# Silu of the values' compressor from Exp and VectorE operations, and one weight load queued behind the first copy of compressed keys, in a transformer block

## The chip, the cores and the metric

The kernel runs on one core of a Trainium2 chip. The core has TensorE (PE in the profile; its weight loads are listed apart as PEld), VectorE (DVE), ScalarE (ACT), GpSimd (POOL) and SyncE (SP), whose queue issues most DMAs. The metric is the device time of one execution in microseconds (us). Before the change the median of 3 runs is 960.73 us (960.63 to 961.4).

## The reference

One layer of a "macaron" transformer on 512 tokens of width 1024, all in float32:

- x = x + 0.5 * swiglu(rmsnorm(x)), a feed-forward part with hidden width 2816;
- x = x + mixer(rmsnorm(x)), the attention part;
- x = x + 0.5 * swiglu(rmsnorm(x)), and a last rmsnorm.

The mixer projects x to queries, keys and values of two families of eight heads. The first family (MoBA, heads 0 to 7 in the kernel) attends causally. The second (NSA, heads 8 to 15) adds three attentions under gates: over selected blocks, over a window, and over compressed keys and values. The compressor is what the change touches:

```
def compress(raw, pos, w1, w2):
    blocks = raw[:, :, idx] + pos
    return jax.nn.silu(blocks.reshape(B, G, n_cmp, NSA_CMP_LEN * dh) @ w1) @ w2

k_cmp = compress(kc_raw, pos_k, w1_k, w2_k)
v_cmp = compress(vc_raw, pos_v, w1_v, w2_v)
```

It is run once for the keys and once for the values: windows of 32 tokens, a hidden layer of 256, Silu, and a second matrix to 64 columns. Silu(h) is h / (1 + exp(-h)).

## The kernel before

Activations lie transposed, features on the partitions, in eight tiles of 128x512. Each float32 matrix product is made of three products of rounded halves: a value is split into a rounded copy (hi, by a Copy on ScalarE, line 95 for weights) and the rest (lo, by a subtraction on VectorE or GpSimd, lines 97 and 99), and `mm3` (lines 106 to 108) multiplies hi by hi, hi by lo and lo by hi.

The program has three phases: the first feed-forward part, the mixer and the second feed-forward part. The change is in the mixer. There two kinds of work are woven together by hand:

- Attention steps: logits of one head (line 1070), softmax (lines 1078 to 1087: sum with the bias and row minimum on VectorE, Exp on ScalarE, reciprocal of the sum on VectorE, scaling on GpSimd), transposes of the probabilities (line 1106) and the product with the values (lines 121 and 122).
- A stream of jobs that need a weight, such as the projections. The list `pre` is worked off before the attention begins, `fill` between its steps. `pre` ends with ... `ksec[1], nq[0], *vhid, nq[1]` and `fill` begins with `vsec[0], mq[0], vsec[1], nq[2]`. Here ksec and vsec are the second halves of the compressors of keys and values, vhid the values' hidden layer, nq and mq the projections of the queries of the NSA and MoBA heads. Within `stream`, `taken` loads up to three jobs ahead of the one that is worked on: `load` (line 75) fills one of four buffers `raw` by a DMA from SP, and `halves` splits it.

`need(("n", 1))` runs the stream until the query projection nq[1] is in; then the attention steps begin, and `run` advances the stream between them at a fixed rate.

What sets the order on each engine: the program is traced in the order of the Python code, and at the build a scheduler orders the instructions of each engine by a timeline of its own, the earlier in the program the sooner. `tc.issue_after(x)` adds an ordering edge: the instructions traced inside it, those on the same engine as x, come behind x on that engine. `held` uses it to keep the stream's matmuls behind the latest attention matmul. SP's queue, as each engine's, is worked off in order; an issue that waits holds what stands behind it.

In `compress`, `hidden` ends with lines 863 to 865: hid is the sum of two halves of the product in PSUM (a Copy on ScalarE, then the sum on VectorE), and Silu is applied on ScalarE, in place, on 64x256. ScalarE has tables for its functions, and the trace shows an ACT_TABLE_LOAD where a function needs another table. `turned` transposes hid on TensorE (line 874) and splits it (lines 880 and 881). `second` makes the second product; for the keys it writes the compressed keys of both groups into kst and copies them to the other 64 partitions by DMA, two copies for each group (lines 898 and 899, SP). kst[0] and kst[2], of the first group, are read by the logits of heads 8 to 11, kst[1] and kst[3] by those of heads 12 to 15. For the values it builds a tile vc and copies it by three DMAs (line 915).

The query of a head, aq, is made by lines 721 (ScalarE) and 722 (VectorE) from the scaled projection (line 715). Tiles with the tag "t" (scaled projections, hid, the lo half of the turned hid) share six buffers.

Of the kernel before, what the change touches and what calls it, by code (L numbers as in the profile page):

```python
# [9 lines left out]
F32 = mybir.dt.float32  # L10
F32R = mybir.dt.float32r
AF = mybir.ActivationFunctionType
ALU = mybir.AluOpType
# [16 lines left out]
def block_kernel(ctx: ExitStack, tc: tile.TileContext, A: dict, out: bass.AP):  # L30
# [7 lines left out]
    nc = tc.nc  # L38
# [16 lines left out]
    def f32(ap):  # L55
        return ap.bitcast(F32)
# [12 lines left out]
    def chunk(shape):  # L69
        raw = wp.tile([128, 1024], F32, name="raw", tag="raw", bufs=4)  # L70
        return raw[:, :shape[0] * shape[1]].rearrange("p (a b) -> p a b", a=shape[0])

    def load(src):
        v = chunk(src.shape[1:])
        nc.sync.dma_start(v, src)
        return halves(v, 48 if src.shape[-1] == HT else 0)
# [537 lines left out]
    with ExitStack() as ph:  # L614
        tmp = ph.enter_context(tc.tile_pool(name="tmp1", bufs=5))
# [64 lines left out]
    with ExitStack() as ph:  # L680
        tmp = ph.enter_context(tc.tile_pool(name="tmp2", bufs=2))
# [3 lines left out]
        def half(i):  # L685
            return slice(i * 64, i * 64 + 64)
# [23 lines left out]
        def scaled(p, by):  # L710
            t = tmp.tile([128, S], F32, name="t", tag="t", bufs=6)
            if by is None:
                nc.vector.tensor_tensor(t, p, R, ALU.mult)
            else:
                nc.vector.scalar_tensor_tensor(t, p, by, R, ALU.mult, ALU.mult)
            return t
# [94 lines left out]
                return src[:, k0:k1], body  # L811
            return [chunk_of(k0) for k0 in range(0, NK, per)]

        vm = []

        def vm_tiles():
            if not vm:
# [7 lines left out]
        def compress(which):  # L825

            xc, p = [], []
            tag = ("t", "mm")[which]

            def blocks(p):  # L830
                tv = scaled(p, None).rearrange("p (n s) -> p s n", s=16)
                xt = chunk((16, 64))
                xv = xt.rearrange("p l (g n) -> p l g n", g=2)
                nc.gpsimd.memset(xv[:, :, :, 31:32], 0.0)
                for g in range(2):
                    for l in range(2):
                        for e in range(2):
                            nc.vector.tensor_tensor(
                                xv[half(l), 8 * e:8 * e + 8, g, 0:31], tv[half(g), l:16:2, e:e + 31],
                                pos[half(g), which, 16 * e + l:16 * e + 16:2].unsqueeze(2).to_broadcast([64, 8, 31]),  # L840
                                ALU.add)
                for l0 in range(0, 16, 4):
                    t = akt().rearrange("p (l e n) -> p l e n", l=4, e=2)
                    nc.scalar.activation(t[:, :, 0], xt[:, l0:l0 + 4], AF.Copy)
                    nc.vector.tensor_tensor(t[:, :, 1], xt[:, l0:l0 + 4], f32(t[:, :, 0]), ALU.subtract)
                    xc.extend(t[:, l].rearrange("p e n -> p (e n)") for l in range(4))

            def hidden(c):
                def body(w):
                    if c == 0:  # L850
                        p.append(pt("mm", "pc"))
                    for l in range(4):
                        x, n = xc[c + l], c + l
                        with held():
                            if n:
                                nc.tensor.matmul(p[0][:64, :256], x[:, :64], w[l][1], start=False, stop=False)
                            newest[0] = nc.tensor.matmul(p[0][:, :256], x, w[l][0], start=n == 0, stop=n == 15)
                            if not n:
                                nc.tensor.matmul(p[0][:64, :256], x[:, :64], w[l][1], start=False, stop=False)
                        yield  # L860
                    if c == 12:
                        hid = tmp.tile([64, 256], F32, name="hid", tag="t", bufs=6)
                        nc.scalar.activation(hid, p[0][64:, :256], AF.Copy)
                        nc.vector.tensor_tensor(hid, p[0][:64, :256], hid, ALU.add)
                        nc.scalar.activation(hid, hid, AF.Silu)
                        p.append(hid)
                return A["w1"][which][:, c:c + 4], body

            def turned(w):
                hid = p[1]  # L870
                pp = pt(tag, "pct")
                for c in range(2):
                    with held():
                        nc.tensor.transpose(pp[:, c * 64:(c + 1) * 64], hid[:, c * 128:(c + 1) * 128],
                                            ident[:64, :64])
                yield
                hh = tmp.tile([128, 2, 64], F32R, name="hh", tag="hh", bufs=1)
                hl = tmp.tile([128, 2, 64], F32R, name="hl", tag="t", bufs=6)
                pv = pp[:, :128].rearrange("p (a b) -> p a b", a=2)
                nc.scalar.activation(hh, pv, AF.Copy)  # L880
                nc.vector.tensor_tensor(hl, pv, f32(hh), ALU.subtract)
                p.append((hh, hl))

            def second(w):
                hh, hl = p[2]
                pp = pt(tag, "pck")
                if which == 0:
                    for c in range(2):
                        with held():
                            mm3(pp[:64, :64], w[c], (hh[:, c], hl[:, c]), c == 0, c == 1)  # L890
                    yield
                    lo, hi = slice(0, CK), slice(CK, 2 * CK)
                    for g in range(2):
                        v, h, l = pp[:64, g * CK:(g + 1) * CK], kst[g], kst[2 + g]
                        nc.scalar.activation(h[0:64, hi], v, AF.Copy)
                        for to in (l[0:64, hi], h[0:64, lo]):
                            nc.vector.tensor_tensor(to, v, f32(h[0:64, hi]), ALU.subtract)
                        nc.sync.dma_start(f32(h[64:128, :2 * CK]), f32(h[0:64, :2 * CK]))
                        nc.sync.dma_start(f32(l[64:128, hi]), f32(l[0:64, hi]))
                    got["kc"] = True  # L900
                    return
                for g in range(2):
                    b = slice(g * 32, (g + 1) * 32)
                    for c in range(2):
                        with held():
                            mm3(pp[:32, g * 64:(g + 1) * 64], (hh[:, c, b], hl[:, c, b]), w[c], c == 0, c == 1)
                yield
                pv = pp[:32, :128].rearrange("p (a b) -> p a b", a=2)

                a = kv.tile([128, 2, 2, 2, 64], F32R, name="vc")  # L910
                nc.gpsimd.memset(f32(a), 0.0)
                nc.scalar.activation(a[:32, 0, :, 0], pv, AF.Copy)
                nc.vector.tensor_tensor(a[:32, 0, :, 1], pv, f32(a[:32, 0, :, 0]), ALU.subtract)
                for r, odd in ((2, 0), (1, 1), (3, 1)):
                    nc.sync.dma_start(f32(a[r * 32:(r + 1) * 32, odd]), f32(a[0:32, 0]))
                got["vc"] = a

            return (proj(8 + which, blocks), [hidden(c) for c in range(0, 16, 4)],
                    ((None, turned), (A["w2"][which], second)))
# [26 lines left out]
        def stream(jobs, ahead=3):  # L946

            jobs, loaded = list(jobs), []

            def taken():  # L950
                while jobs and len(loaded) <= ahead:
                    src, body = jobs.pop(0)
                    loaded.append((None if src is None else load(src), body))
                w, body = loaded.pop(0)
                return body(w), body

            while jobs or loaded:
                steps, body = taken()
                if body not in [job[1] for job in swapped]:
                    yield from steps  # L960
                    continue
                for _ in range(NK - 1):
                    next(steps)
                    yield
                more, _ = taken()
                for one in (more, steps):
                    next(one)
                    latest[0] = newest[0]
                    yield
                yield from steps  # L970
                yield from more
# [207 lines left out]
        mq, mk = [[proj(2 * i + j, moba_t(kind, i)) for i in range(4)] for j, kind in enumerate("qk")]  # L1179
# [71 lines left out]
    with ExitStack() as ph:  # L1251
        tmp = ph.enter_context(tc.tile_pool(name="tmp3", bufs=5))
# [201 lines left out]
```

## Time and profile before

| what | value |
| --- | --- |
| median of 3 runs | 960.73 us (960.63 to 961.4) |
| profiled execution, its own time | 960.46 us |
| its span, from the first to the last instruction | 958.7 us |
| PE, PEld, DVE, ACT, POOL busy | 949.7, 879.8, 764.6, 563.2, 163.2 us |
| mean granted TensorE clock | 0.998 |
| table loads on ScalarE, all and in the stretch from 383 to 425 us | 11 and 4, 1.28 us each |

All other times are those of the profiled execution, in us from the start of its span. "L865" is line 865 of the kernel before. In a timeline row stand the start, the duration, the engine, the line, the operation, the output and inputs by the program's names, the shape and the number of merged instructions (the duration is then that of all of them together, and the name that of the first); in brackets the idle time of the engine just before and what ended it. An engine with a q is its sequencer, so SPq rows are the issues of DMAs. In a row by lines stand the count, the busy time in all, the mean duration of one in ns and the idle time before. The durations of matmuls overlap, because they are pipelined.

### The profile page before, as it was taken

What the parts mean: (1) busy time and instruction counts of PE and PEld (TensorE: products, weight loads), DVE (VectorE), ACT (ScalarE), POOL (GpSimd) and SP (SyncE); (2) the same over time, 40 slices, a digit from 0 to 9 for tenths busy, and PEclk for the clock granted to TensorE, in tenths of its full rate; (3) what the DMA queues carried; (4) which work ended last, traced back from release to release, by engine and by line L of the source; (5) the groups of instructions that cost most, each with busy time, mean ns of one, the idle gap of its engine ahead of it and who ended that gap; (6) DMA issues with size and microseconds to landing.
All of it is one profiled execution on the core that took longest, in us unless ns stands there. A gap on an engine that the chain in (4) does not pass through costs nothing.

```text
span 958.7 us, 18276 instructions
## 1 busy us (share of the span) xinstructions
PE 949.7 (99%) x6703; PEld 879.8 (92%) x6703; DVE 764.6 (80%) x1596; ACT 563.2 (59%) x1170; POOL 163.2 (17%) x209
## 2 busy tenths in 40 slices
PE   9999999999999999999999999999999999999997
PEld 7889999999999989889888888888999999999985
DVE  7998897688777588967788677889889788778954
ACT  6565555454554356778877887655565545545443
POOL 2000000000000000056778897100000000000002
PEclk9999999999999999999999999999999999999999
DMA  8447444333321226551312332236334321425442
GB/s 283 128 166 235 140 133 135 113 92 95 106 68 57 60 67 179 163 160 35 90 38 72 92 96 73 66 106 224 130 114 132 131 79 56 133 51 123 92 154 88
DMA packets 70138, 109.17 MB, mean 114 GB/s; under 512 B 27518, under 2 KB 34127, under 8 KB 70049
## 3 DMA queue, kind: packets, MB, share of 16 engines
q1 hardware_dynamic: 69232, 106.68, 36.1%
q8 instruction: 52, 0.85, 0.4%
q0 software_dynamic: 384, 0.55, 0.3%
q10 hardware_dynamic: 432, 0.79, 0.2%
q14 instruction: 38, 0.30, 0.1%
HBM read 100.44 MB, written 7.40 MB: 112 GB/s over the span
## 4 chain that ended last, share of the span: by engine, by line
PE 97%; DVE 1%; DMA 1%; ACT 0%; issue 0%; POOL 0%; POOLq 0%; SPq 0%; DVEq 0%; ACTq 0%
PE pd L116 14%; PE pu L108 7%; PE pu L106 7%; PE pu L107 7%; PE pw L106 5%; PE pw L108 5%; PE pw L107 5%; PE pd L107 4%; PE pd L108 4%; PE pd L106 4%; PE ps_s L1070 3%; PE pgu L107 3%; PE pgu L108 3%; PE pgu L106 3%; PE pp L106 3%; PE pp L108 3%
## 5 line engine op out<-in xcount | busy, mean ns | idle before, releaser
L249 ACT ACTIVATE sph<-aw 128x512 fp32r<-128x512 f32 x252 | 157.9, 631 | 193.7 <-issue 71.9
L250 DVE TENSOR_TENSOR spl<-aw,sph 128x512 fp32r<-128x512 f32 x252 | 171.2, 684 | 55.2 <-ACT sph L249 53.3
L95 ACT ACTIVATE whi<-raw 128x512 fp32r<-128x512 f32 (+2 forms) x198 | 119.2, 614 | 85.0 <-PE pd L116 25.3
L116 PE MATMUL pd<-h,whi 128*128 128x256 f32 x784 | 120.7, 276 | 0.0
L99 DVE TENSOR_TENSOR wlo<-raw,whi 128x512 fp32r<-128x512 f32 (+1 forms) x162 | 106.8, 669 | 16.1 <-ACT whi L95 15.9
L108 PE MATMUL pu<-th,spl 128*128 128x256 f32 x432 | 119.3, 276 | 0.0
L106 PE MATMUL pu<-th,sph 128*128 128x256 f32 x432 | 119.2, 276 | 0.0
L107 PE MATMUL pu<-tl,sph 128*128 128x256 f32 x432 | 119.2, 276 | 0.0
L116 PEld LDWEIGHTS pd<-h,whi 128*128 128x128 f32 x784 | 103.5, 188 | 0.1
L335 DVE TENSOR_TENSOR aw<-aw 128x512 f32<-128x512 f32 x144 | 98.2, 682 | 0.0
L106 PEld LDWEIGHTS pu<-th,sph 128*128 128x128 f32 x432 | 81.1, 188 | 1.3
L107 PEld LDWEIGHTS pu<-tl,sph 128*128 128x128 f32 x432 | 81.1, 188 | 1.2
L108 PEld LDWEIGHTS pu<-th,spl 128*128 128x128 f32 x432 | 81.1, 188 | 0.0
L108 PE MATMUL pw<-xo,spl 128*128 128x256 f32 x288 | 79.6, 276 | 0.0
L106 PE MATMUL pw<-xo,sph 128*128 128x256 f32 x288 | 79.4, 276 | 0.0
L107 PE MATMUL pw<-xo,sph 128*128 128x256 f32 x288 | 79.4, 276 | 0.0
L116 PE MATMUL pd<-h,wlo 128*128 128x256 f32 x392 | 76.3, 276 | 0.0
L612 DVE SCALAR_TENSOR_TENSOR x<-pd,x 128x512 f32<-128x512 f32 x80 | 54.3, 682 | 14.7 <-PE pd L116 12.4
L1354 POOL TENSOR_SCALAR mean<-ss 128x1 f32<-128x1 f32 x4 | 1.4, 343 | 343.5 <-ACT sqd L1314 343.4
L116 PEld LDWEIGHTS pd<-h,wlo 128*128 128x128 f32 x392 | 59.0, 188 | 0.0
L991 POOL MEMSET tb<- 128x256 f32 x16 | 4.9, 312 | 311.4 <-DVE x L612 310.4
L106 PEld LDWEIGHTS pw<-xo,sph 128*128 128x128 f32 x288 | 54.1, 188 | 1.7
(271 smaller groups left out, 2707.3 us busy)
## 6 DMA issues: line engine op xcount, KB each, us to landing
aw<-in_wg SPq DMA_DIRECT2D x72, 256.0 KB, 4.3
aw<-in_wu SPq DMA_DIRECT2D x72, 256.0 KB, 4.8
raw<-in_wd1a SPq DMA_DIRECT2D x20, 512.0 KB, 3.9
raw<-in_w_a SPq DMA_DIRECT2D x16, 512.0 KB, 3.7
raw<-in_wd2a SPq DMA_DIRECT2D x16, 512.0 KB, 3.6
raw<-in_w SPq DMA_DIRECT2D x8, 512.0 KB, 4.7
raw<-in_w_o SPq DMA_DIRECT2D x8, 512.0 KB, 3.6
raw<-in_wg SPq DMA_DIRECT2D x7, 512.0 KB, 3.5
```

Of the source, the lines that this page charges most:

```text
L95: last_hi[0] = nc.scalar.activation(hi, v, AF.Copy)
L99: nc.vector.tensor_tensor(lo, v, f32(hi), ALU.subtract)
L106: nc.tensor.matmul(p, w[0], v[0], start=first, stop=False, skip_group_check=again)
L107: nc.tensor.matmul(p, w[0], v[1], start=False, stop=False, skip_group_check=again)
L108: newest[0] = nc.tensor.matmul(p, w[1], v[0], start=False, stop=last, skip_group_check=again)
L116: nc.tensor.matmul(p[:, h], a, b[:, h], start=first and n + i == 0, stop=last and n == 2, skip_group_check=True)
L249: nc.scalar.activation(hi, v, AF.Copy)
L250: self.last_lo = nc.vector.tensor_tensor(lo, v, f32(hi), ALU.subtract)
L335: nc.vector.tensor_tensor(to, x, y, op)
L612: nc.vector.scalar_tensor_tensor(xs[d], p, 0.5, xs[d], ALU.mult, ALU.add)
L991: nc.gpsimd.memset(t[:, :S - 256], 0.0)
L1070: latest[0] = nc.tensor.matmul(to, q, k, start=part == at, stop=part != at)
```

## The change

Two edits. First, for the values' compressor alone (which == 1) Silu is no longer one operation of ScalarE: ScalarE makes e = exp(-h) into a new tile of the tag "t", and VectorE adds 1, takes the reciprocal and multiplies by h. The keys' compressor keeps Silu. Second, the issue of the first copy of line 899 that is traced (first group) is remembered, and the load of the weight of mq[0], the first query projection of the MoBA heads, is traced inside `issue_after` of it: the DMA of this load then stands behind that copy on SP's queue. The operations that split the weight, on other engines, get no such edge.

```
--- before.py
+++ after.py
@@ -811,7 +811,7 @@
                 return src[:, k0:k1], body
             return [chunk_of(k0) for k0 in range(0, NK, per)]
 
-        vm = []
+        vm, kc_copied = [], [None]
 
         def vm_tiles():
             if not vm:
@@ -862,7 +862,14 @@
                         hid = tmp.tile([64, 256], F32, name="hid", tag="t", bufs=6)
                         nc.scalar.activation(hid, p[0][64:, :256], AF.Copy)
                         nc.vector.tensor_tensor(hid, p[0][:64, :256], hid, ALU.add)
-                        nc.scalar.activation(hid, hid, AF.Silu)
+                        if which == 0:
+                            nc.scalar.activation(hid, hid, AF.Silu)
+                        else:
+                            e = tmp.tile([64, 256], F32, name="e", tag="t", bufs=6)
+                            nc.scalar.activation(e, hid, AF.Exp, scale=-1.0)
+                            nc.vector.tensor_scalar(e, e, 1.0, None, ALU.add)
+                            nc.vector.reciprocal(e, e)
+                            nc.vector.tensor_tensor(hid, hid, e, ALU.mult)
                         p.append(hid)
                 return A["w1"][which][:, c:c + 4], body
 
@@ -896,7 +903,8 @@
                         for to in (l[0:64, hi], h[0:64, lo]):
                             nc.vector.tensor_tensor(to, v, f32(h[0:64, hi]), ALU.subtract)
                         nc.sync.dma_start(f32(h[64:128, :2 * CK]), f32(h[0:64, :2 * CK]))
-                        nc.sync.dma_start(f32(l[64:128, hi]), f32(l[0:64, hi]))
+                        copied = nc.sync.dma_start(f32(l[64:128, hi]), f32(l[0:64, hi]))
+                        kc_copied[0] = kc_copied[0] or copied
                     got["kc"] = True
                     return
                 for g in range(2):
@@ -950,7 +958,8 @@
             def taken():
                 while jobs and len(loaded) <= ahead:
                     src, body = jobs.pop(0)
-                    loaded.append((None if src is None else load(src), body))
+                    with tc.issue_after(kc_copied[0].ins) if body is mq[0][1] else nullcontext():
+                        loaded.append((None if src is None else load(src), body))
                 w, body = loaded.pop(0)
                 return body(w), body
 
```

More of the change, by code (lines that the diff above doesn't have):

```diff
@@ L812, in token_major @@
             return [chunk_of(k0) for k0 in range(0, NK, per)]
-        vm = []
+        vm, kc_copied = [], [None]
         def vm_tiles():
@@ L864, in body @@
                         nc.vector.tensor_tensor(hid, p[0][:64, :256], hid, ALU.add)
-                        nc.scalar.activation(hid, hid, AF.Silu)
+                        if which == 0:
+                            nc.scalar.activation(hid, hid, AF.Silu)
+                        else:
+                            e = tmp.tile([64, 256], F32, name="e", tag="t", bufs=6)
+                            nc.scalar.activation(e, hid, AF.Exp, scale=-1.0)
+                            nc.vector.tensor_scalar(e, e, 1.0, None, ALU.add)
+                            nc.vector.reciprocal(e, e)
+                            nc.vector.tensor_tensor(hid, hid, e, ALU.mult)
                         p.append(hid)
@@ L898, in second @@
                         nc.sync.dma_start(f32(h[64:128, :2 * CK]), f32(h[0:64, :2 * CK]))
-                        nc.sync.dma_start(f32(l[64:128, hi]), f32(l[0:64, hi]))
+                        copied = nc.sync.dma_start(f32(l[64:128, hi]), f32(l[0:64, hi]))
+                        kc_copied[0] = kc_copied[0] or copied
                     got["kc"] = True
@@ L952, in taken @@
                     src, body = jobs.pop(0)
-                    loaded.append((None if src is None else load(src), body))
+                    with tc.issue_after(kc_copied[0].ins) if body is mq[0][1] else nullcontext():
+                        loaded.append((None if src is None else load(src), body))
                 w, body = loaded.pop(0)
```

## The prediction

> **What bounds the kernel now.** I read the page first, for the engine that sets the end.
>
> ```profile
> span 958.7 us, 18276 instructions
> PE 949.7 (99%) x6703; PEld 879.8 (92%) x6703; DVE 764.6 (80%) x1596; ACT 563.2 (59%) x1170; POOL 163.2 (17%) x209
> ...
> PE 97%; DVE 1%; DMA 1%; ACT 0%; issue 0%; POOL 0%; POOLq 0%; SPq 0%; DVEq 0%; ACTq 0%
> ```
>
> TensorE (PE) is busy for 99% of the span and makes up 97% of the chain that ended last. The change touches VectorE (DVE), ScalarE (ACT) and a DMA, so it can move the end only where PE waits for one of them. The second view is busy time by stretch, over the stage and over the 10 us around the edit.
>
> ```profile
> core 0: us, PE busy (x) PEld busy (x) DVE busy (x) ACT busy (x) POOL busy (x), PEclk, DMA share, GB/s
> 404.00:414.00 10.00, 9.63 (x54) 8.11 (x53) 8.46 (x26) 9.89 (x19) 2.19 (x3) 1.00 0.62 185
> 300.00:600.00 300.00, 299.63 (x1882) 267.33 (x1882) 223.16 (x632) 210.14 (x488) 148.80 (x186) 1.00 0.32 92
> ```
>
> Of 300 us around the change PE is idle for 0.37 us, all of it in these 10 us. (Short losses between overlapping matmuls don't show as idle time.) ACT is almost full there, 9.89 of 10.00 us: a place crowded on ACT, where PE hardly waits. The third view, the chain of waits, says what the idle 0.37 us is.
>
> ```profile
> 400.70 3.87 DMA kst<-kst
> 404.57 0.14 issue
> 404.71 1.18 PE ps_s L1070 x6
> ```
>
> The first attention logits (L1070) wait for the first copy of compressed keys to land, at 400.70 + 3.87 = 404.57. This is the wait at which the moved load aims.
>
> **The moved load.** SP's queue in time, with the landings of the load at 400.27 and of three small copies that ran later (L915), and what VectorE did for the logits:
>
> ```profile
> 400.27 0.33 SPq L75 DMA_DIRECT2D raw<-in_w_a  x1
> 400.70 0.47 SPq L898 DMA_DIRECT2D kst<-kst  x1
> 401.22 0.59 SPq L899 DMA_DIRECT2D kst<-kst  x1
> ...
> 402.51 0.59 SPq L899 DMA_DIRECT2D kst<-kst  x1
> ```
>
> ```profile
> DMA to landing us min/median/max: 4.1/4.1/4.1
> ```
>
> ```profile
> DMA to landing us min/median/max: 1.9/1.9/1.9
> ```
>
> ```profile
> 400.16 0.27 DVE L897 TENSOR_TENSOR kst<-pck,kst 64x32 fp32r<-64x32 f32 x2
> ...
> 403.62 0.69 DVE L722 TENSOR_TENSOR aq<-t,aq 64x512 fp32r<-64x512 f32 x1
> ```
>
> The load at 400.27 is mq[0]'s, the last of the stream's loads before vsec[1]'s. It is 512 KB, issued just ahead of the copies, and it lands at 400.27 + 4.1 = 404.4; the copy behind it lands 0.2 us later. Behind the copies it delays them no more. Their data are there at 400.16 + 0.27 = 400.43, so the first could be issued at about 400.5 instead of 400.70. Landing then takes between the 1.9 us of the L915 copies and the 3.87 us of now; I take the lower end, since the 4.1 us neighbour is gone: about 402.4, at worst 404.4. The logits have a second condition, though: their weights are aq, and L722 ends at 403.62 + 0.69 = 404.31. So the wait ends at 404.31, not at 402.4, and the gain is 404.57 - 404.31 = 0.26 us (0.2 at the slow landing). Not below nothing: nothing is added ahead of the copies.
>
> What moves with the load: one DMA issue of 0.33 us, past two of the copies or all four. It would start at about 401.7 (400.5 and the two issues of 0.47 and 0.59, with their gaps) or at 402.9, and land near 405.8 or 407.0. The second group's copies, if the load slips in ahead of them, come 0.33 us later; they feed the last four heads only, so that costs nothing. Two ACT copies and two DVE subtractions split what it brings; they are weighed below. vb's second load takes the same buffer after that split and comes up to 2.6 us later (407.0 - 404.4); its matmuls are queued behind all of mq[0]'s, which hide it.
>
> **The Silu.** ACT and VectorE around it, then PE and GpSimd (POOL):
>
> ```profile
> 403.80 2.71 ACT L95 ACTIVATE whi<-raw 128x512 fp32r<-128x512 f32 x5
> 406.53 1.28 ACT L1080 ACT_TABLE_LOAD   x1
> ...
> 409.92 0.61 ACT L95 ACTIVATE whi<-raw 128x512 fp32r<-128x512 f32 x1
> 410.55 1.28 ACT L865 ACT_TABLE_LOAD   x1
> 411.85 0.42 ACT L865 ACTIVATE hid<-hid 64x256 f32<-64x256 f32 x1
> 412.28 1.28 ACT L1080 ACT_TABLE_LOAD   x1
> ```
>
> ```profile
> 409.58 0.40 DVE L864 TENSOR_TENSOR hid<-pc,hid 64x256 f32<-64x256 f32 x1
> ...
> 410.57 0.88 DVE L99 TENSOR_TENSOR wlo<-raw,whi 128x512 fp32r<-128x512 f32 x1 [0.16 <-ACT whi L95]
> 411.37 0.68 DVE L1078 CUSTOM_DVE_ANT_0 lp<-ps_s,tb 128x512 f32<-128x512 f32 x1
> ...
> 412.43 0.69 DVE L715 SCALAR_TENSOR_TENSOR t<-pp,R 128x512 f32<-128x512 f32 x1 [0.37 <-PE pp L108]
> ```
>
> ```profile
> 412.23 0.27 PE L1106 MATMUL ps_t<-ident,lpn 128*128 128x128 f32 x1
> ...
> 412.89 0.33 PE L874 MATMUL pct<-ident,hid 64*128 64x64 f32 x2
> ...
> 414.00 0.40 PE L106 MATMUL pp<-xo,whi 128*128 128x512 f32 x1
> ```
>
> ```profile
> 409.78 2.20 POOL L1087 TENSOR_SCALAR lpn<-lpn,m,gates 128x128 f32<-128x128 f32 x3 [24.02 <-DVE m L1082]
> ```
>
> Removed: two table loads, 2 x 1.28 = 2.56 us of ACT, since Exp's table is in from 406.53 on. Who waits for them? hid is ready at 411.85 + 0.42 = 412.27 and PE takes it at 412.89 (L874), 0.62 us later: nobody on PE. So by these rows the removal alone is worth nothing at the end.
>
> Added on VectorE: an add, a reciprocal and a product, 64x256 each. Their nearest rows, by line with shapes kept apart:
>
> ```profile
> L240 DVE TENSOR_TENSOR xc<-xa 128x256 f32<-128x256 f32 x8 | 3.3, 414 | 0.0
> L1142 DVE TENSOR_SCALAR mc<-mc 128x8 f32<-128x8 f32 x4 | 1.0, 246 | 0.0
> L1323 DVE TENSOR_SCALAR xo<-x,ss 128x512 f32<-128x512 f32 x1 | 0.5, 474 | 0.0
> L1082 DVE RECIPROCAL m<-m 128x1 f32<-128x1 f32 x96 | 14.0, 154 | 10.1 <-ACT lp L1080 4.9 <-ACT lpn L1080 4.9
> L1147 DVE RECIPROCAL mc<-mc 128x8 f32<-128x8 f32 x4 | 0.8, 197 | 0.0
> ```
>
> The product is L240's 0.41. The add lies between 0.25 (8 columns) and 0.47 (512); I take 0.33. The reciprocal of 256 columns isn't in the trace. [...] Against that, 8 columns take 197 ns and one takes 154: 43 ns / 7 = 6.1 ns a column, and 154 + 255 x 6.1 = 1.71 us. I take 1.71, because it is drawn from the instruction itself. [...]
>
> So hid in the new kernel: the sum ends at 409.58 + 0.40 = 409.98. Exp needs 0.42 (the Silu's row; no table load), and starts at 409.98 or behind the copy at 409.92, at 410.53: done at 410.40 or 410.95. Then 0.33 + 1.71 + 0.41, less the 0.08 by which neighbours on VectorE overlap (L99 ends at 411.45, L1078 starts at 411.37) twice: 2.29 us. hid is ready at 412.69 or 413.24 with nothing in between. PE, 0.26 us earlier by the first part, is at L874 at 412.63: it waits 0.06 or 0.61 us. I take 0.6, since ACT is full and the copy stands first. [...] Queued on PE behind L874 are transposes, logits and mq[0]'s matmuls, thus everything: a wait there is paid in full.
>
> VectorE itself is held 2.3 us. Behind it stand L99 for a weight that is not next, L1078 for logits lp and L715. They have cover from 414.00 on, where mq[0]'s 24 matmuls need none of them. The new tile is one more user of six shared buffers; the last older one, nq[0]'s scaled tile, is read out by L722: nothing.
>
> **Sum**, on the profiled execution (960.46 us for a span of 958.7; median of the runs 960.73, so 0.27 above): -0.26 + 0.6 = +0.34 us, 960.80; in the frame of the medians 961.1. That is 0.04%. A measurement of this kernel can tell about 0.2%, 1.92 us, from no change.
>
> **Rivals.**
>
> *Nothing waits for hid.* The build's scheduler orders each engine; if it puts other PE work ahead of L874, or runs Exp at once, only the gain is left: -0.26, at most -0.37 with all idle time gone, 960.5. For it: mq[0]'s matmuls are free to go first. Against: its order must know the reciprocal's length.
>
> *The reciprocal chain is cut up (slower).* L99, L1078 and L715 stand on VectorE between 410.57 and 413.12 now. If they keep their places between the new operations, they add 0.88 + 0.68 + 0.69 less three overlaps of 0.08 = 2.01: hid at 413.24 + 2.01 = 415.25, a wait of 2.6, the end +2.4: 963.1. It decides from a hid later than 412.63 + 0.26 + 1.92 = 414.81. For it: no operation there is idle work. Against: hid is older in the program than L1078 and L715.
>
> *The late load holds ACT.* mq[0]'s two copies are the last of the five from 403.80, due at 403.80 + 3 x 0.54 = 405.4. With its landing at 405.8 or 407.0 ACT would stand 0.4 or 1.6 us, and with it Exp and POOL's L1087. That ends at 409.78 + 2.20 = 411.98, and L1106 on PE starts at 412.23 and would start at 411.97: no slack is left. End: -0.26 + 0.26 + 0.4 to 1.6, up to 962.3. Even without a stop, L1087 may take back the gained 0.26. Against: the scheduler can put the Exps ahead of the copies.
>
> *The table loads were on the path after all (faster).* 960.73 - 2.56 = 958.2. Against: no PE idle time after 404.71 in the stretch. [...]
>
> **How the numbers follow.** Forecast (a short wait at L874) 0.42; nothing waits 0.31; cut up 0.12; ACT held 0.11; loads on the path 0.04. Faster by over 0.2%: the last, and 0.01 for a luckier order, 0.05. Slower by over 0.2%: 0.10 of the cut-up case and 0.04 of the held one, 0.14. Same: 0.81. The range runs from 960.0 (nothing waits, less 0.5, about the spread of the runs, 960.63 to 961.4) to 962.8, which holds all of the held case and the milder cut.
>
> **What would show it.** Right: two table loads fewer in the stage; a RECIPROCAL of 64x256 near 1.7 us; kst's first copy landing well before 404; L1070 released by aq of L722; PE idle just before L874. Wrong: a reciprocal near 0.4 us; a kst copy still landing at 404.5; or PE idle time elsewhere, above all before L1106 with ACT waiting on raw. A change over 2 us either way means that the scheduler laid the stage anew, which these rows can't price.

## The result, and the profile after

The changed kernel takes 967.24 us (median of 6 runs, 966.38 to 967.84); the kernel before, on the same chip, 960.75 us (6 runs, 960.63 to 961.42). The ratio is 1.0064, with a 95% interval of 1.0052 to 1.0077. The forecast was 961.1 us in a range of 960.0 to 962.8: the change costs 6.5 us where 0.3 us were forecast. The profiled execution took 967.84 us, with a span of 965.9 us against 958.7.

The page of the changed kernel, its lines on engines and on the chain that ended last:

```profile
span 965.9 us, 18281 instructions
...
PE 953.9 (99%) x6703; PEld 881.3 (91%) x6703; DVE 769.4 (80%) x1599; ACT 560.3 (58%) x1168; POOL 164.7 (17%) x209
...
PE 97%; DMA 1%; DVE 1%; ACT 1%; POOL 0%; issue 0%; SPq 0%; POOLq 0%; ACTq 0%; DVEq 0%
```

By shares nothing has happened. PE has as many matmuls as before (6703), yet is *busy* 4.2 us longer (953.9 against 949.7). More busy time for the same work is the first sign that something made the matmuls themselves slower. The stretches of busy time place it, first in the changed kernel, then in the kernel before (busy time and count of each engine, then the granted clock, PEclk):

```profile
404.00:430.00 26.00, 22.89 (x108) 17.77 (x108) 18.79 (x60) 16.06 (x40) 9.47 (x13) 0.87 0.43 130
430.00:500.00 70.00, 70.00 (x456) 62.82 (x453) 53.42 (x194) 51.64 (x135) 48.95 (x62) 1.00 0.25 70
```

```profile
404.00:430.00 26.00, 25.63 (x145) 21.70 (x144) 18.68 (x64) 21.48 (x49) 12.54 (x16) 1.00 0.51 153
```

In the 26 us around the edit PE is idle for 26.00 - 22.89 = 3.11 us instead of 0.37, and its mean clock is 0.87, which is worth 26 x 0.13 = 3.4 us. So 2.7 us of waiting and 3.4 us of lost clock, together 6.1 of the 7.2 us between the two spans. Of the 1.1 us that are left, 0.5 were lost ahead of the stage (the split of aq, L722, starts at 404.12 instead of 403.62); where the rest went is not shown. From 430 to 500 PE is busy all the time, at the full clock.

PE in time in the changed kernel (start, duration, line, tile, shape, count; in brackets the idle time before and what ended it):

```profile
414.22 0.62 PE L1079 MATMUL ps_s<-kvn,aq 128*128 128x384 f32 x2 [0.46 <-DVE m L1087]
417.36 0.98 PE L1079 MATMUL ps_s<-kvn,aq 128*128 128x512 f32 x2 [2.52 <-DVE m L1087]
418.44 0.69 PE L1115 MATMUL ps_t<-ident,lp 128*128 128x128 f32 x2
...
419.97 0.47 PE L881 MATMUL pct<-ident,hid 64*128 64x64 f32 x2
420.37 0.79 PE L106 MATMUL pp<-xo,whi 128*128 128x512 f32 x1
...
423.95 0.63 PE L108 MATMUL pp<-xo,wlo 128*128 128x512 f32 x1
424.37 0.45 PE L106 MATMUL pp<-xo,whi 128*128 128x512 f32 x1
```

L1079 is the logits (L1070 before), L1115 the transposes of probabilities (L1106), L881 the transposes of hid (L874). The wait is not at L881, where the prediction had put it, but ahead of two groups of logits: 0.46 and 2.52 us, ended both times by L1087 on VectorE, the bias sum of the softmax, which reads logits and so empties their PSUM bank. mq[0]'s matmuls, 24 in one row from 414.00 on in the kernel before, begin at 420.37, *behind* L881. And they take 0.63 us each until 423.95 and 0.39 or 0.40 soon after: that is the halved clock, 0.51 granted from 417.60 to 424.50. In the kernel before the same 128x512 logits came only when mq[0] was through:

```profile
419.26 0.39 PE L108 MATMUL pp<-xo,wlo 128*128 128x512 f32 x1
...
419.95 0.71 PE L1070 MATMUL ps_s<-kvn,aq 128*128 128x512 f32 x2
```

Who held L1087? VectorE in time, changed kernel:

```profile
413.48 0.68 DVE L1087 CUSTOM_DVE_ANT_0 lp<-ps_s,tb 128x512 f32<-128x512 f32 x1
...
414.09 0.28 DVE L870 TENSOR_SCALAR e<-e 64x256 f32<-64x256 f32 x1
414.40 1.75 DVE L871 RECIPROCAL e<-e 64x256 f32<-64x256 f32 x1
416.07 0.62 DVE L715 SCALAR_TENSOR_TENSOR t<-pp,R 128x512 f32<-128x512 f32 x1
...
416.88 0.41 DVE L1087 CUSTOM_DVE_ANT_0 lpn<-ps_s,tb 128x256 f32<-128x256 f32 x1
417.23 0.07 DVE L1087 DVE_READ_ACCUMULATOR2_ANT m<- 128x1 f32 x1
...
418.31 0.41 DVE L872 TENSOR_TENSOR hid<-hid,e 64x256 f32<-64x256 f32 x1
```

The reciprocal stands between two sums of L1087. The second ends at 417.30 and PE goes on at 417.36. The last step of the chain, the product, comes at 418.31, behind L715 and three sums; hid is ready at 418.72.

L715, which also stands behind the reciprocal, holds the cover itself. It reads the projection nq[1] and so empties its PSUM bank. nq[1], the transposes of hid and mq[0] share a tag with two banks. In the kernel before, mq[0]'s matmuls begin at 414.00, while the bank of the transposes is still read (by line 881 of the kernel before, a subtraction):

```profile
415.92 0.28 DVE L881 TENSOR_TENSOR hl<-pct,hh 128x128 fp32r<-128x128 f32 x1
```

So mq[0] takes the other bank, nq[1]'s. In the changed kernel it couldn't have begun before L715 ends, at 416.07 + 0.62 = 416.69, even if it had stood ahead of the transposes: only the last 417.36 - 416.69 = 0.67 us of the wait were open to it.

The chain of waits puts the steps in one column:

```profile
403.30 3.99 DMA raw<-in_w_a
...
407.94 0.61 ACT whi L95
408.57 1.28 ACT L1089
...
412.61 0.95 DVE wlo L99
413.56 0.60 DVE lp L1087
414.40 1.75 DVE e L871
416.15 0.54 DVE t L715
416.86 1.54 POOL lp L1096
418.44 0.69 PE ps_t L1115 x2
```

Before, this chain ran over PE from 404.71 on. Now it leaves PE: from the moved load over ScalarE's weight copies and its table load, VectorE's sum, the reciprocal and GpSimd's scaling, back to PE at 418.44.

### The profile page after: what moved, and what is told of

Same layout as the page of the kernel before. It is cut to its first block, busy times and chain, and to the rows that moved or that the text cites. A ratio compares the mean times of both kernels' runs of the same rounds, so it can differ in the third digit from the quotient of the medians.

```text
span 965.9 us, 18281 instructions
## 1 busy us (share of the span) xinstructions
PE 953.9 (99%) x6703; PEld 881.3 (91%) x6703; DVE 769.4 (80%) x1599; ACT 560.3 (58%) x1168; POOL 164.7 (17%) x209
## 4 chain that ended last, share of the span: by engine, by line
PE 97%; DMA 1%; DVE 1%; ACT 1%; POOL 0%; issue 0%; SPq 0%; POOLq 0%; ACTq 0%; DVEq 0%
PE pd L116 14%; PE pu L108 7%; PE pu L106 7%; PE pu L107 7%; PE pw L106 5%; PE pw L108 5%; PE pw L107 5%; PE pd L107 4%; PE pd L108 4%; PE pd L106 4%; PE ps_s L1079 3%; PE pp L106 3%; PE pgu L107 3%; PE pgu L108 3%; PE pgu L106 3%; PE pp L108 3%
## 5 line engine op out<-in xcount | busy, mean ns | idle before, releaser
L99 DVE TENSOR_TENSOR wlo<-raw,whi 128x512 fp32r<-128x512 f32 (+1 forms) x162 | 106.6, 667 | 18.9 <-ACT whi L95 18.6
```

The lines of the kernel that those rows point to most:

```text
L99: nc.vector.tensor_tensor(lo, v, f32(hi), ALU.subtract)
```

## Experiments

Each is told by its difference to the changed kernel unless said otherwise. "Before" is the kernel before on the same chip in the same batch: 961.63 us (median of 26 runs) for the load alone, the Silu alone, no reciprocal and mq[0]'s product in other banks, 961.1 us (27 and 23 runs) for the others.

The expectations of those four name three theories. Theory A: the reciprocal holds VectorE in front of the work that frees the banks of the logits, while mq[0]'s matmuls, which covered this place, stand behind hid. Theory B: the late load alone costs the time, by holding ScalarE. Theory C: the reciprocal alone costs it.

**The load alone.** The Silu is put back:

```
-                        if which == 0:
-                            nc.scalar.activation(hid, hid, AF.Silu)
-                        else:
...
+                        nc.scalar.activation(hid, hid, AF.Silu)
```

> Only the load of mq[0] behind the first copy; Silu stays on ScalarE. Theory A: ScalarE stands for the landing of the weight, the values' Silu with its table load ends about 414.3 instead of 412.3, PE waits some 1.4 us for hid, 962 us, clock not halved. Theory B: 967 us with the clock halved. Theory C: 960.5 us, the small gain of the earlier copy.

Measured: 961.96 us, ratio 1.0003 (0.9994 to 1.0012). The clock stays at 1.0. PE in this run:

```profile
414.41 0.34 PE L874 MATMUL pct<-ident,hid 64*128 64x64 f32 x2 [0.94 <-ACT hid L865]
```

The late load does hold ScalarE, for 1.32 us, and with it hid, which PE now awaits for 0.94 us. The rest of PE's order is as before, and the time can't be told from the before of its batch, as theory A expected. The load alone doesn't explain the result.

**The Silu alone.** The load stays where it was:

```
-                    with tc.issue_after(kc_copied[0].ins) if body is mq[0][1] else nullcontext():
-                        loaded.append((None if src is None else load(src), body))
+                    loaded.append((None if src is None else load(src), body))
```

> Exp and VectorE operations as in the changed kernel, the load of mq[0] where it was before. Theory A (the reciprocal holds VectorE in front of the work that frees the PSUM banks of the logits, and mq[0]'s matmuls, which covered this place, stand behind hid on PE; the late load adds 2 us on ScalarE; the idle time then halves the clock): PE waits some 1.4 us for the softmax behind the reciprocal and less for lp, 962.7 us, and up to 967 if the clock is halved again. Theory B (the late load alone does it, by holding ScalarE): 960.7 us, as before. Theory C (the reciprocal alone does it): 967 us with the clock halved.

Measured: 963.73 us (median of 5, 963.63 to 966.52), ratio 1.0034 (1.0020 to 1.0048). The five runs fall in two groups: 966.52 and 966.27 with mean clocks of 0.996 and 0.997, and 963.63, 963.71 and 963.73 with 0.998 to 0.999. The profiled one is of the first group:

```profile
415.67 0.73 PE L1078 MATMUL ps_s<-kvn,aq 128*128 128x512 f32 x2 [1.67 <-DVE m L1086]
416.75 0.69 PE L1114 MATMUL ps_t<-ident,lp 128*128 128x128 f32 x2 [0.35 <-POOL lp L1095]
```

The Silu alone brings the new order and the wait for L1086 (L1087 in the changed kernel); with the one for GpSimd's scaling behind it, 2.02 us, where theory A had expected some 1.4. Against the before of its batch it costs 2.1 us, and in some executions 2.7 us more by the clock. The load, harmless alone, makes the waits longer (0.46 + 2.52 in place of 1.67 + 0.35), and all six runs of the changed kernel show a mean clock of 0.995 to 0.997.

**No reciprocal.** The one line is taken out:

```
-                            nc.vector.reciprocal(e, e)
```

> The changed kernel without the one reciprocal of 64x256 (the values' hidden layer is then h times (1 + exp(-h)) and not Silu). Theory A: mq[0]'s matmuls stand behind hid, which comes 1.75 us sooner, about 414.5; PE waits 0.5 to 1 us, clock not halved: 961.5 us. Theory B: 967 us, since the late load is still there. Theory C: 960.6 us.

Measured: 961.96 us, ratio 1.0002 (0.9993 to 1.0011), clock 1.0. Here the hidden layer is h times (1 + exp(-h)). L880 (hid's transposes) stands at 415.13, ahead of mq[0] and of the 128x512 logits again. mq[0]'s first matmul then waits for L715, which shows that it needs the bank that L715 empties:

```profile
415.64 0.50 PE L106 MATMUL pp<-xo,whi 128*128 128x512 f32 x1 [0.20 <-DVE t L715]
```

So nearly all of the loss needs the reciprocal. But taking it out also changed PE's order, so this run can't say whether its length or the order costs the time.

**Half the reciprocal.** Only 128 of the 256 columns are divided. Here PE's order stays that of the changed kernel as far as the transposes behind the 128x512 logits:

```
-                            nc.vector.reciprocal(e, e)
+                            nc.vector.reciprocal(e[:, :128], e[:, :128])
```

> The changed kernel with the reciprocal taken over 128 of its 256 columns alone; the other half is left undivided, so that pass should take about 0.9 us in place of 1.75. TensorE's order is that of the changed kernel up to the transposes of hid. The theory of VectorE's hold expects the wait ahead of the 128x512 logits to shrink by the same 0.87 us, from 2.52 to about 1.65; then the idle time costs 3.0 - 0.87 = 2.1 us and the time is 963.0 to 963.5 us if the clock keeps up, and 966.3 us if 1.65 us of waiting still halves it. The theory that the order alone costs the time, and not how long VectorE is held, expects 967 us.

Measured: 964.73 us (median of 6, 963.41 to 968.17), ratio 1.0042 (1.0025 to 1.0058). VectorE and PE in the profiled run:

```profile
415.10 0.95 DVE L871 RECIPROCAL e<-e 64x128 f32<-64x128 f32 x1
```

```profile
417.25 0.73 PE L1079 MATMUL ps_s<-kvn,aq 128*128 128x512 f32 x2 [1.71 <-DVE m L1087]
```

The operation is shorter by 1.75 - 0.95 = 0.80 us, the wait by 2.52 - 1.71 = 0.81. In this order the reciprocal is paid by PE one to one. The time lies above the 963.0 to 963.5 that was expected for a full clock. The executions differ: one of 968.17 us has a mean clock of 0.995. But the profiled one, 964.75 us, kept its clock and is over 963.5 as well; in its trace the first logits start at 405.85 in place of 404.86, so about 1 us of it was lost ahead of the stage.

**mq[0]'s product in other banks.** The reciprocal and the late load stay; only the PSUM tag of the first query projection of the MoBA heads changes, from the one that the transposes of hid use as well:

```
-                p = pt("mm", "pp")
+                p = pt("o" if i == 0 else "mm", "pp")
```

> The changed kernel with mq[0]'s projection in a PSUM bank of the tag o instead of mm, so that its 24 matmuls needn't come behind the transposes of hid. Theory A: they cover the reciprocal and the late ScalarE, PE hardly waits and the clock stays up: 960.6 to 961.5 us. Theories B and C, if the wait is ScalarE's or VectorE's own and no cover helps: still over 965 us.

Measured: 962.0 us, ratio 1.0007 (0.9997 to 1.0016), clock 1.0; theory A's 960.6 to 961.5 us are missed by 0.5. VectorE, then PE:

```profile
414.41 1.75 DVE L871 RECIPROCAL e<-e 64x256 f32<-64x256 f32 x1
```

```profile
408.09 0.50 PE L106 MATMUL pp<-xo,whi 128*128 128x512 f32 x1 [1.02 <-ACT whi L95]
...
419.10 0.97 PE L1079 MATMUL ps_s<-kvn,aq 128*128 128x128 f32 x6
```

The reciprocal has the same length at the same place, and costs nothing. But this isn't the order of the kernel before. To judge by the wait for its weight at 408.09, mq[0] now runs ahead of nearly all of nq[1], whose matmuls then run beside the reciprocal, and the first window logits, at 412.62 in the changed kernel, come at 419.10. So the missing cover was the other half of the cause. Whether mq[0] lacked it by its place behind the transposes or by the bank that L715 empties, this run can't say: the new tag takes away both. What is left is a wait of 1.02 us for the late load, which mq[0], further ahead now, reaches too soon.

**The same, load not moved.** The Silu alone (as above) with the other banks.

> The Silu from Exp as in the change, the load left where it was, and mq[0]'s matmuls in the other group of banks. The theory that the cost lay in the missing cover and not in the reciprocal's 1.75 us expects the reciprocal at its full length and the time of the kernel before, 960.5 to 961.5 us; the theory that the reciprocal costs by itself expects the 963.7 to 966.5 us of the Exp form alone.

Measured: 960.98 us, ratio 0.9999 (0.9991 to 1.0008). VectorE, then all that PE waited for between 404 and 430:

```profile
412.38 1.75 DVE L871 RECIPROCAL e<-e 64x256 f32<-64x256 f32 x1
```

```profile
404.76 0.97 PE L1078 MATMUL ps_s<-kst,aq 128*128 128x160 f32 x5 [0.35 <-DMA kst<-kst]
```

With other matmuls beside it again, in the order of the run before, the Exp form is as fast as the kernel before, and not faster: two table loads fewer bring nothing that can be measured.

**The clock.** Is the halved clock a loss of its own? Eleven matmuls whose result nothing uses are put ahead of the waiting logits, behind the 128x384 group, in a bank that is free:

```
+                if h == 8 and kind == "kw" and qis == (2,):
+                    warm = pt("o", "warm")
+                    for _ in range(11):
+                        with held():
+                            latest[0] = nc.tensor.matmul(warm, xg[0][0][:, :128], xg[0][0], start=True, stop=True)
```

> The changed kernel with eleven matmuls of 128x512 added, whose result nothing uses, on TensorE directly behind the second group of window logits (128x384 x2), ahead of the group of 128x512 that waited 2.52 us; they take a bank that is free there. At 0.227 us each they fill 2.5 us, and TensorE's other work stands in the same order as in the changed kernel. The reciprocal, the order and the late load are all left in. If the halved clock is caused by the idle time, and is a loss of its own, the clock stays at 1.0 and 3.4 us come back: 967.2 - 3.4 = 963.8 us (963.3 to 964.3), with the logits still starting at about 417.4 in the trace. If the halved clock is not caused by that idle stretch, or if it costs nothing because the work behind it waits anyway, the time stays at 967 us or a little above.

Measured: 964.94 us (median of 4, 964.85 to 965.92), ratio 1.0039 (1.0026 to 1.0053). PE, and its busy time in the stretch where the clock had been halved, first for the changed kernel and then for this one:

```profile
414.35 2.69 PE L1084 MATMUL warm<-xo 128*128 128x512 f32 x11
417.03 0.73 PE L1079 MATMUL ps_s<-kvn,aq 128*128 128x512 f32 x2
```

```profile
417.60:424.50 6.90, 6.80 (x20) 4.85 (x20) 5.51 (x22) 4.82 (x16) 3.47 (x6) 0.51 0.32 95
```

```profile
417.60:424.50 6.90, 6.54 (x32) 5.25 (x32) 5.18 (x21) 5.04 (x17) 4.06 (x8) 1.00 0.33 95
```

The logits start no sooner, yet PE does 32 matmuls instead of 20 in the same 6.9 us. Filling an idle gap with useless work gives back 3.0 us of span (965.9 to 962.9), and 2.3 us between the medians. So the lost clock is a loss of its own, and a wait brought it on. The 963.8 us that were expected are missed by 1.1.

**Four of them instead of eleven:**

```
-                    for _ in range(11):
+                    for _ in range(4):
```

> The kernel with the added matmuls, four of them in place of eleven (0.9 us in place of 2.5; their result is used by nothing): about 1.6 us of the wait ahead of the 128x512 logits stays, in TensorE's unchanged order. Time by the waits alone is that of eleven, 964.9 us. If 1.6 us without work, beside the waits of 0.5 us ahead of it and behind it, is enough to halve the clock, it is 967 to 968 us; if a stretch nearly as long as the 2.5 us is needed, 964.9 us with the clock at 1.0.

Measured: 964.91, 965.83, 966.06 and 968.67 us; ratio 1.0054 (1.0039 to 1.0070). The profiled run, 964.91 us, kept the clock at 1.0 with this wait:

```profile
417.14 0.73 PE L1079 MATMUL ps_s<-kvn,aq 128*128 128x512 f32 x2 [1.59 <-DVE m L1092]
```

The last run, 3.8 us longer, has a mean clock of 0.996 against 0.998. If the lower means come from this stretch, which no kept trace shows, some 1.6 us of idle time halve the clock in some executions and not in others. The question of a threshold gets no clean answer.

**A shorter hold.** Silu(h) is also h/2 times 1 + tanh(h/2): one function on ScalarE and one pass on VectorE, with the factor 1/2 in the copies of the compressed values. With the load moved:

```
+                            nc.scalar.activation(e, hid, AF.Tanh, scale=0.5)
+                            nc.vector.scalar_tensor_tensor(hid, e, 1.0, hid, ALU.add, ALU.mult)
...
+                nc.scalar.activation(a[:32, 0, :, 0], pv, AF.Copy, scale=0.5)
+                nc.vector.scalar_tensor_tensor(a[:32, 0, :, 1], pv, 0.5, f32(a[:32, 0, :, 0]), ALU.mult, ALU.subtract)
```

> The changed kernel, but the Silu made from one Tanh on ScalarE and one pass on VectorE (h times one plus tanh of h/2; the factor 1/2 goes into the copies of the compressed values), with the load moved. VectorE holds about 0.4 us in place of 2.4, so the theory that the reciprocal's hold on VectorE costs the time expects no wait of 2.5 us, no halved clock, and 961.5 to 962.3 us, as with the load moved alone (961.96) or a bit less. If Tanh can stay in the table that Exp uses there are two table loads fewer than before; if it can't, their number is as before and hid comes 1.3 us later, still covered in part. The theory that any form made on both engines reorders the stage expects 964 us or more.

Measured: 961.71 us, ratio 1.0005 (0.9997 to 1.0014). ScalarE and VectorE:

```profile
408.04 1.28 ACT L1087 ACT_TABLE_LOAD   x1
...
411.95 0.40 ACT L869 ACTIVATE e<-hid 64x256 f32<-64x256 f32 x1
413.66 0.72 ACT L1087 ACTIVATE lp<-lp,m 128x512 f32<-128x512 f32 x1 [1.31 <-DVE m L1085]
```

```profile
413.55 0.41 DVE L870 SCALAR_TENSOR_TENSOR hid<-e,hid 64x256 f32<-64x256 f32 x1
```

No table is loaded between Tanh (L869, at 411.95) and the Exps around it: the one load from 400 to 420 stands at 408.04. VectorE is held 0.41 us, hid's transposes stay ahead of mq[0] and of the 128x512 logits, and the loss is gone with the late load still in.

The Tanh form with the load left alone:

> The Tanh form with the load left where it was. The theory of VectorE's hold expects the kernel before or slightly better: 960.7 to 961.6 us, its wait at the transposes of hid gone or smaller, two table loads fewer if Tanh shares the table of Exp. The theory that the two steps of the change cost by themselves, whatever VectorE holds, expects 963 to 966 us as with the Silu alone changed to Exp (963.7 or 966.4).

Measured: 961.3 us, ratio 1.0001 (0.9992 to 1.0009). And with mq[0] in the other banks as well:

> The Tanh form with the load left where it was, and the first of the projections behind the stage (mq[0]) written to the other group of banks, so that its 24 matmuls don't stand behind the transposes of hid. The theory that TensorE lacked cover because of that order expects no wait over 0.1 us between 404.9 and 430, and the best time of all forms: what the kernel before has of waits in the stage (0.37 us at 404.5) stays, so 960.3 to 961.2 us. If the order was no part of the loss, it equals the Tanh form without it.

Measured: 960.87 us, ratio 1.0000 (0.9991 to 1.0009); behind the first logits, at 404.88, PE is never idle up to 430. All three parts together, load included:

> All that was found, together: the Silu from Tanh, the load moved, mq[0]'s matmuls in the other group of banks. If the waits add up, the wait ahead of the first logits falls to 0.2 us as with the load moved, there is none at the logits behind it, and the time is 960.2 to 961.0 us. If the load, now wanted earlier by matmuls that stand further ahead, is late for them (it cost a wait of 1.19 us in the changed kernel with these banks), it is 961.5 to 962.2 us.

Measured: 962.08 us, ratio 1.0010 (1.0002 to 1.0019). The second of the two expectations holds; PE waits for the late weight:

```profile
408.07 0.50 PE L106 MATMUL pp<-xo,whi 128*128 128x512 f32 x1 [0.85 <-ACT whi L95]
```

No version beats the kernel before by what can be measured. The idle 0.37 us of the prediction's second view was all the idle time that PE had to give here.

## Why the prediction was wrong

Its single durations and its first part were right; the step that failed is the one that decided. The prediction's own last sign came true: a change over 2 us means that the scheduler laid the stage anew.

- *The first wait.* Right in its mechanism. kst's copies no longer hold the logits; they start at 404.86, when the first split of aq on VectorE is through. The gain of 0.26 us can't be seen as time, since aq itself came 0.5 us later than in the trace before.
- *The moved load.* Right in size. It was issued at 403.30, behind all four copies (402.9 had been the later estimate), ScalarE stood 1.43 us for it (0.4 to 1.6), and Exp's table came at 408.57 in place of 406.53. As a rival this was priced at up to 962.3; alone it gave 961.96.
- *The table loads.* Right: two fewer, and worth nothing (960.98 with the Exp form and mq[0] in the other banks).
- *The Silu's sizes.* Right: the reciprocal took 1.75 us (1.71 from the slope of two small rows), the add 0.28 (0.33), the product 0.41.
- *Where hid is ready.* Wrong: 418.72, not 413.24. Part of it is the late load: the sum of hid ended at 411.22 instead of 409.98, Exp at 412.88 instead of 410.95, and the add came behind L99 and a sum of L1087, at 414.09. The prediction had weighed the load and the Silu each by itself, and here they add up. Then L715 and three sums of L1087 came ahead of the product, which is the rival "cut up" (415.25) and more. Yet PE's wait wasn't for hid.
- *The step that failed:* "They have cover from 414.00 on, where mq[0]'s 24 matmuls need none of them." One of the three operations meant there is L715, and mq[0]'s matmuls do need it: it empties their PSUM bank (the wait of 0.20 us without the reciprocal). Behind the reciprocal it ended at 416.69 instead of 413.12. Besides, with hid late, its transposes moved behind the next logits on PE and mq[0] with them, to 420.37. So the 2.3 us for which VectorE was held, put at nothing in the sum, had no cover: ahead stood only logits that need a bank which VectorE empties, with the reciprocal queued in front, and PE waited 2.52 us. The other banks for mq[0] (same reciprocal, 962.0 and 960.98 us) show that the hold costs nothing where PE has other matmuls; the half reciprocal (0.80 us shorter, wait 0.81 shorter) shows that it is paid in full where it has none.
- *What stood in no step:* that 2.7 us more of idle time on PE brought on a halved clock (0.51 over 6.90 us), which is worth another 3.4 us by the trace.

The theory that the load alone was at fault fell with the first experiment. That the reciprocal alone was at fault holds only in the new order. How much of the missing cover is L715's bank and how much the place behind the transposes stays open, since no run changed one without the other. Why the scheduler moved the transposes is argued and not shown: its timeline is in no trace, but they moved with a reciprocal, whole or half, and stayed with the Silu, without the reciprocal and with Tanh. Open stays, too, which executions lose their clock.

## What to carry to other kernels

Cover is only cover if it can start: before counting work that stands *behind* an edit as what hides it, ask which operations it waits for (here the one that empties its PSUM bank), whether one of them stands on the engine that the edit holds, and what fixes its place in its own engine's order, since it may move away with the edited step. When an operation moves from an engine with room to one that frees another's banks, price it as a hold on everything that engine owes, with no cover as the bad end of the range. And where TensorE is the bound, look for the clock behind a wait: in the profiled runs here, waits of 1.67 and 2.52 us had a halved clock behind them (0.51 over 6.90 us), which is worth 3.4 us by the trace, and waits of 1.59 and 1.71 us had not.

## What the runs showed of the hardware

**The clock.** In the changed kernel the granted clock went to one half behind the waits of 0.46 and 2.52 us and came back. The stretches ahead of the drop, in it and behind it:

```profile
416.00:417.60 1.60, 0.24 (x1) 0.25 (x2) 1.60 (x8) 0.85 (x2) 0.74 (x1) 1.00 0.01 5
417.60:424.50 6.90, 6.80 (x20) 4.85 (x20) 5.51 (x22) 4.82 (x16) 3.47 (x6) 0.51 0.32 95
424.50:430.00 5.50, 5.50 (x36) 4.63 (x35) 1.22 (x4) 1.68 (x3) 3.59 (x4) 1.00 0.00 0
```

In the profiled run of the Silu alone, with a wait of 1.67 us ending at 415.67, it was as low over a stretch of the same length:

```profile
416.60:423.50 6.90, 6.75 (x19) 5.33 (x20) 4.83 (x21) 4.17 (x15) 2.78 (x6) 0.51 0.37 103
```

With half the reciprocal, whose wait took 1.71 us, and with four added matmuls, where it took 1.59 us, the clock was 1.00 from 414 to 430 in the profiled runs. So the length of the longest wait doesn't tell by itself whether the clock drops; what else decides it is not shown.

**The reciprocal.** 128 columns took 0.95 us and 256 took 1.75: 0.80 us / 128 = 6.3 ns a column, beside the 6.1 that the prediction had from 1 and 8 columns. In the changed kernel the reciprocal of 64x256 took over four times as long as VectorE's product of the same shape (0.41).
